# Second layer of a decoder trunk: earlier pools and loads, a one-step residual, and a later addition of R1

## The chip, the cores and the metric

The kernel runs on one core of a Trainium2 chip. The core has five engines, each with its own queue that runs in order: TensorE (PE; its weight loads are shown apart as PEld), VectorE (DVE), ScalarE (ACT), GpSimd (POOL) and SyncE (SP), which here only sends DMAs. The metric is the device time of one execution in microseconds, the median of several runs.

## The reference

A trunk of two layers over x of 512 positions by 1024 features, all in float32. Each layer is a mixer and a feed-forward part, each behind a residual and a layer norm:

```python
for layer in range(DEPTH):            # DEPTH = 2
    ...                               # layer 0: state space + stick-breaking attention; layer 1: convolution module
    x = layer_norm(DEEPNORM_ALPHA * x + mix, ln1_g[layer], ln1_b[layer])
    ffn = sqrelu_mlp(x, ffn_w1[layer], ffn_b1[layer], ffn_w2[layer], ffn_b2[layer])
    x = layer_norm(DEEPNORM_ALPHA * x + ffn, ln2_g[layer], ln2_b[layer])

def sqrelu_mlp(x, w1, b1, w2, b2):
    return jnp.square(jax.nn.relu(x @ w1 + b1)) @ w2 + b2
```

The change touches the feed-forward part of layer 1 and the norm ahead of it. There `x @ w1` has 4096 outputs, and `@ w2` goes back to 1024.

## The kernel before

Activations lie transposed, features on the 128 partitions: `X[0]` to `X[7]` are 128 features by 512 positions each. Every float32 product is made of three products of rounded halves (`hi`, `lo`): hi·hi, hi·lo, lo·hi. So each operand has to be converted first: ScalarE rounds it (`whi`, `ah`, `xdh`), VectorE takes the rest (`wlo`, `al`, `xdl`).

**Weights.** The class `Weights` holds a list of units in the order in which TensorE uses them. `_prep` loads a unit and converts it into the next of a ring of slots; `next()` hands one out and prepares a few more ahead (`W.ahead`). Some units were converted during layer 0, kept in DRAM and come back through GpSimd's DMA queue (`split`). When the first unit of the second feed-forward part's second matrix is due (`at_turn`), `turn()` closes the old pools and opens new ones: four slots, buffers for raw weights, and buffers for four quarters (`quad`, loaded by `load_quads`).

**Layer 1's feed-forward part** begins in `tail_norm_lead`. `Tail` forms the residual sums ahead of the norm, `ln_to_x` normalises the 512 positions in two halves and splits the result into `xdh`/`xdl`, and `Lead` runs the first six products with `w1` (`fl10` to `fl15`), first for the first half of the positions while the second is still being normalised, and then, in `finish`, for the second half.

Behind that come four blocks of six hidden tiles. In each, `pair` squares two tiles (`q`), forms the sums that a seven-product (Strassen) scheme needs, and splits them (`ah`, `al`). `seven` multiplies them with the four quarters of `w2` and sums of these (`operand` makes the sums on VectorE), seven units of 18 matmuls (`s`) each: 126 matmuls of 512 columns a block. Its results are added to `XT`. The first product goes into `R1[0]` and `R1[1]`, gathered over the four blocks and added to all eight `XT` at the end of the fourth. The last eight hidden tiles take an ordinary product (`h`).

In block 1, ahead of `seven`, `residual` makes alpha·x + b2: it adds `xdh` and `xdl` on VectorE, scales on ScalarE, and turns the eight tiles on TensorE (32 transposes `xt`, copied back by ScalarE), so that the output comes out with positions on the partitions.

A scheduler places each engine's instructions in order ahead of time from the order of the code and what each needs. On the chip each queue then stands at its first instruction until all that this one waits for is done. PSUM has six buffers (`nps`) that leads, transposes and `s` products take in turn.

Of the kernel before, what the change touches and what calls it, by code (L numbers as in the profile page):

```python
# [9 lines left out]
F32 = mybir.dt.float32  # L10
F32R = mybir.dt.float32r
# [5 lines left out]
P = 128  # L17
# [24 lines left out]
NB = 6  # L42
# [16 lines left out]
class Weights:  # L59
# [11 lines left out]
    def fetch(self, i):  # L71
        key, src, nk, ncol, off, width = self.units[i]
        if key not in self.chunk:
            tag, bufs = (f"quad{i % 2}{i // 2 % 2}", 1) if key[0] == "f21" else ("raw", 2)
            self.chunk[key] = self.raw.tile([P, nk, width], F32, tag=tag, name=f"raw{i}", bufs=bufs)
            self.nc.sync.dma_start(self.chunk[key], src)

    def prep_to(self, n):
# [39 lines left out]
    def load_quads(self, blk, w2, k0, nb):  # L118

        src = w2[k0 * P : (k0 + nb) * P].rearrange("(k e p) (f n) -> e f p k n", e=2, p=P, f=2)  # L120
        q = self.quads[blk] = {}
        for e, f in ((0, 0), (1, 0), (0, 1), (1, 1)):
            q[e, f] = self.raw.tile([P, nb // 2, T], F32, tag=f"quad{e}{f}", name=f"quad{blk}{e}{f}", bufs=1)
            self.nc.sync.dma_start(q[e, f], src[e, f])

    def operand(self, blk, i):
# [70 lines left out]
def kernel(ctx: ExitStack, tc: tile.TileContext, a: dict, out: bass.AP):  # L197
# [831 lines left out]
    class Lead:  # L1029


        def __init__(self, n, xs, name):
            self.n, self.xs, self.name, self.held = n, xs, name, []

        def run(self, n):
# [8 lines left out]

        def finish(self):
            self.run(self.n - len(self.held))
            n, (c0, c1) = TOGETHER.get(self.name, 0), HALVES[1]
            for k, (xh, xl) in enumerate(self.xs):
                for (hi, lo), ps in self.held[:n]:
                    for i, (u, v) in enumerate(((hi, xh), (hi, xl), (lo, xh))):  # L1050
                        PE.matmul(ps[:, c0:c1], u[:, k, :], v[:, c0:c1], start=k == 0 and i == 0, stop=k == KT - 1 and i == 2)
            for w, ps in self.held[n:]:
                gemm(ps, w, slice(0, P), self.xs, c0, c1)
            W.prep_to(W.got + 2)
            W.fence = None
            return [ps for _, ps in self.held]

    def tail_norm_lead(xk, name, bias, g, b, lead_n, lead_name, then=None):
# [7 lines left out]
        lead = Lead(lead_n, xs, lead_name)  # L1066
# [23 lines left out]
        return hs  # L1090


    rb = [const([P, KT], "rb0"), res_bias("rb1", ("ln1_b", 0), ("ffn_b2", 0)), res_bias("rb2", ("ln2_b", 0), ("conv_b_pw2", 0))]
    for n in ("ln1_g", "ln2_g", "conv_ln_g"):
        c = PV[:, vrow[n] : vrow[n] + a[n].shape[0] * KT]
        ts(c, c, -0.5, None, ALU.mult, ALU.bypass)
# [211 lines left out]

    W.ahead = AHEAD[0]

    def turn():
        wst.close()
        pools = [ctx.enter_context(tc.tile_pool(name=f"w3{x}", bufs=1, reuse_waits="tile")) for x in "abc"]
        W.slots, W.base, W.raw, W.ahead = [], W.done, pools[1], NSLOT - 1
        W.add_slots(pools[0], 2)
        W.add_slots(pools[2], NSLOT - 2)
        W.load_quads(0, a["ffn_w2"][1], 0, NB)

    W.turn = (at_turn, turn)
    xs, first = tail_norm_lead(cs_, "d", None, ("ln1_g", 8), ("ln1_b", 8), LEAD, "fl1", the_rest)  # L1320


    XT = [None] * KT
# [1 line left out]

    def residual():
        for j in range(KT):
            tt(X[j], xs[j][0].bitcast(F32), xs[j][1].bitcast(F32), ALU.add)
            act(X[j], X[j], AF.Identity, bias=pv("ffn_b2", 8 + j), scale=ALPHA)
        for f in range(2):  # L1330
            pss = [nps(f"xt{b}{f}") for b in range(4)]
            for b in range(4):
                for i in range(4):
                    PE.transpose(pss[b][:, i * P : (i + 1) * P], X[4 * f + i][:, b * P : (b + 1) * P], ident)
            for b in range(4):
                XT[2 * b + f] = X[4 * f + b]
                S.copy(X[4 * f + b], pss[b])

    hst.close()
    f1 = ctx.enter_context(tc.tile_pool(name="f1", bufs=1, side="right", reuse_waits="tile"))  # L1340
    R1 = [page(f"R1{t}", F32) for t in range(2)]

    def rect(m, ps):
# [32 lines left out]
    def seven(blk, As, first, final):  # L1376

        bank = {}
        for i in ORDER7:
# [24 lines left out]

    k0 = 0
    for bi, nb in enumerate(FFN_BLOCKS[1][:-1]):
# [5 lines left out]
        seven(k0, As, bi == 0, bi == len(FFN_BLOCKS[1]) - 2)  # L1412
        k0 += nb
    hs = []
    for i in range(nb_last):
        if i % 3 == 0:
            hl_ = [f1.tile([P, 3, T], F32R, tag=f"a{x}", name=f"b{x}{i}", bufs=NB // 2) for x in "hl"]
# [20 lines left out]
    sts = [f1.tile([P, 2, 6], F32, tag="bst", name=f"bst{b}", bufs=4) for b in range(4)]  # L1438
    pss = [nps(f"h{b}0") for b in range(4)]
    for k in range(nb_last):  # L1440
        if k % 3 == 0:
# [10 lines left out]
    ws = [W.next() for _ in range(-(-nb_last // 3))]  # L1452

    def block(b):
        mv = f1.tile([P, 4], F32, tag="bmv", name=f"bmv{b}", bufs=2)
        ps = nps(f"h{b}1")
        for k in range(nb_last):
            part(ps, b, k, ws[k // 3])
# [47 lines left out]
```

## Time and profile before

| | us |
|---|---|
| median of 3 runs (1172.56 to 1175.39) | 1173.91 |
| the profiled execution, its own time | 1172.98 |
| its span, first to last instruction | 1171.2 |
| PE busy | 1138.9 (97%) |
| PEld busy | 953.1 (81%) |
| DVE busy | 822.9 (70%) |
| ACT busy | 551.7 (47%) |

Times in the profile count from the span's start. Line numbers (L110) are those of the kernel before. Matmuls are pipelined and their ends are modelled, so a busy PE is not one at its peak; what counts is the distance between starts, and the idle time with the instruction that ended it. "Granted clock" is the share of TensorE's full clock. A view of windows gives the busy time of each engine in a stretch that the reader chooses.

### The profile page before, as it was taken

To read this page: it belongs to the slowest core of one execution; us is meant where nothing else is said; L and a number is where in the kernel's file an instruction comes from. 1 tells how busy PE (TensorE), PEld (TensorE's weight loads), DVE (VectorE), ACT (ScalarE), POOL (GpSimd) and SP (SyncE) were. 2 spreads that over 40 slices of the span, in tenths; PEclk is the share of its full clock that TensorE was granted. 3 is DMA by queue.
4 is the path that set the end of the run, shared out by engine and by line. 5 is a ranking of instruction groups with operands and counts; after the bars stand their busy time and mean duration, and the time that the engine had idled before them with its cause. 6 is when DMAs were issued, how large, how long until landed. Compare 5 with 4: busy or idle time off the path is not lost.

```text
span 1171.2 us, 17896 instructions
## 1 busy us (share of the span) xinstructions
PE 1138.9 (97%) x7180; PEld 953.1 (81%) x7180; DVE 822.9 (70%) x1396; ACT 551.7 (47%) x838; POOL 67.0 (6%) x125
## 2 busy tenths in 40 slices
PE   9989999999999999999999999899989999999997
PEld 7777767799888888888999777599968888887885
DVE  7999875498646546546555899886785958587337
ACT  7857779345425425425323132662753536363530
POOL 1022210000000000000021110001000000000000
PEclk9999999999999999999999999999989999999999
DMA  8521221332688788788454742206324151514211
GB/s 216 165 56 50 79 85 46 110 116 73 221 286 289 250 287 290 249 286 286 164 177 152 247 144 74 75 9 209 91 79 138 56 151 37 170 36 153 63 55 72
DMA packets 145907, 169.59 MB, mean 145 GB/s; under 512 B 13922, under 2 KB 119138, under 8 KB 145824
## 3 DMA queue, kind: packets, MB, share of 16 engines
q1 hardware_dynamic: 137024, 136.96, 36.7%
q0 software_dynamic: 8640, 31.46, 7.9%
q8 instruction: 56, 0.92, 0.3%
q14 instruction: 27, 0.22, 0.1%
q10 hardware_dynamic: 160, 0.03, 0.0%
HBM read 132.12 MB, written 35.65 MB: 143 GB/s over the span
## 4 chain that ended last, share of the span: by engine, by line
PE 82%; DVE 9%; ACT 4%; issue 2%; DMA 2%; POOL 0%; SPq 0%; DVEq 0%; ACTq 0%; POOLq 0%
PE f L256 24%; PE acf L256 11%; PE s L1390 8%; PE fl L256 5%; PE tlb L256 4%; PE tld L256 4%; PE h L1436 4%; PE pv L256 3%; PE pg L256 3%; PE cw L1165 3%; PE tla L256 2%; PE acmo L256 2%; PE pl L256 2%; DVE wlo L111 1%; PE gg L256 1%
## 5 line engine op out<-in xcount | busy, mean ns | idle before, releaser
L110 ACT CAST whi<-raw 128x1024 fp32r<-128x1024 f32 (+1 forms) x150 | 156.7, 1061 | 257.9 <-PE acf L256 61.0
L111 DVE TENSOR_TENSOR wlo<-raw,whi 128x1024 fp32r<-128x1024 f32 (+1 forms) x150 | 183.8, 1238 | 123.9 <-ACT whi L110 120.5
L256 PE MATMUL f<-xdh,whi 128*128 128x512 f32 x208 | 81.0, 390 | 1.0 <-ACT whi L110 1.0
L256 PE MATMUL f<-xah,whi 128*128 128x512 f32 x208 | 81.1, 390 | 0.0
L256 PE MATMUL f<-xal,whi 128*128 128x512 f32 x208 | 80.9, 389 | 0.0
L256 PE MATMUL f<-xah,wlo 128*128 128x512 f32 x208 | 80.9, 389 | 0.0
L256 PE MATMUL f<-xdl,whi 128*128 128x512 f32 x208 | 80.9, 389 | 0.0
L256 PE MATMUL f<-xdh,wlo 128*128 128x512 f32 x208 | 80.9, 389 | 0.0
L256 PE MATMUL acf<-hh,whi 128*128 128x512 f32 x192 | 75.4, 392 | 0.0
L256 PE MATMUL acf<-hh,wlo 128*128 128x512 f32 x192 | 75.2, 392 | 0.0
L256 PE MATMUL acf<-hl,whi 128*128 128x512 f32 x192 | 74.8, 390 | 0.0
L1390 PE MATMUL s<-whi,ah 128*128 128x512 f32 x168 | 66.0, 400 | 3.3 <-ACT whi L110 2.5
L1390 PE MATMUL s<-wlo,ah 128*128 128x512 f32 x168 | 66.4, 402 | 2.3 <-DVE wlo L111 2.3
L1390 PE MATMUL s<-whi,al 128*128 128x512 f32 x168 | 66.0, 396 | 0.0
L111 DVE TENSOR_TENSOR wlo<-quad,whi 128x1536 fp32r<-128x1536 f32 x28 | 49.0, 1754 | 4.7 <-ACT whi L110 4.4
L110 ACT CAST whi<-quad 128x1536 fp32r<-128x1536 f32 x28 | 41.0, 1478 | 21.9 <-PE f L256 8.0
L389 DVE SCALAR_TENSOR_TENSOR cy<-hp,wdw,cy 128x512 f32<-128x512 f32 (+1 forms) x75 | 49.5, 660 | 0.2 <-ACT cy L185 0.2
L95 POOL DMA_DIRECT2D whi<-kepth x30 | 16.1, 536 | 547.7 <-PE tlb L256 385.5
L256 PEld LDWEIGHTS f<-xdh,whi 128*128 128x128 f32 x208 | 39.0, 188 | 9.4 <-ACT whi L110 1.4
L256 PEld LDWEIGHTS f<-xah,whi 128*128 128x128 f32 x208 | 39.0, 188 | 8.2
L256 PEld LDWEIGHTS f<-xdh,wlo 128*128 128x128 f32 x208 | 39.0, 188 | 8.2
L256 PEld LDWEIGHTS f<-xah,wlo 128*128 128x128 f32 x208 | 39.0, 188 | 8.1
(649 smaller groups left out, 3069.1 us busy)
## 6 DMA issues: line engine op xcount, KB each, us to landing
raw<-in_ffn_w_dram SPq DMA_DIRECT2D x35, 1024.0 KB, 5.6
kepth<-whi SPq DMA_DIRECT2D x30, 512.0 KB, 3.4
keptl<-wlo SPq DMA_DIRECT2D x30, 512.0 KB, 9.4
whi<-kepth POOLq DMA_DIRECT2D x30, 512.0 KB, 3.6
wlo<-keptl POOLq DMA_DIRECT2D x30, 512.0 KB, 4.6
raw<-in_ffn_w_dram SPq DMA_DIRECT2D x28, 512.0 KB, 4.1
raw<-in_conv_w_pw_dram SPq DMA_DIRECT2D x12, 1024.0 KB, 7.3
quad<-in_ffn_w_dram SPq DMA_DIRECT2D x16, 768.0 KB, 4.8
```

What stands on the lines that cost most here:

```text
L95: nc.gpsimd.dma_start(x, d)
L110: i0 = nc.scalar.copy(hi, raw).ins
L111: i1 = nc.vector.tensor_sub(lo, raw, hi.bitcast(F32)).ins
L256: ins = PE.matmul(ps[:, c0:c1], u[:, k, ksl], v[:, c0:c1], start=start and k == 0 and i == 0, stop=stop and k == n - 1 and i == 2).ins
L389: V.scalar_tensor_tensor(o, x, s, y, op0=op0, op1=op1)
L1165: PE.matmul(cps[j, c0][g][C, :], Ds[j][t // 16][R, t % 16, :], hps[j][R, t + c0 : t + c1], start=t < 4, stop=t >= n - 4, tile_position=(R. ...
L1390: PE.matmul(ps, u, v[:, p, :], start=chain == i and p == 0 and n_ == 0, stop=p == len(As) - 1 and n_ == 2, skip_group_check=True)
L1436: PE.matmul(ps, u, v, start=k == 0 and i == 0, stop=k == nb_last - 1 and i == 2)
```

## The change

Five things are done.

- `finish` of the lead prepares three units (`early=3`) ahead of the second half's products instead of two behind them. So `turn()` with its loads is recorded earlier.
- `turn()` now also closes the pool of the convolution's pages (`hst`) and opens all pools of the second feed-forward part at once, over that space too: slots `s1` to `s4`, `raw`, `a0` to `a2` for the split sums, `q`, `b`, and `w` for the quarters. The quarters have a pool of their own, `W.quad`.
- The residual is one ScalarE step from the normalised value before its bias: alpha·y + (alpha·ln1_b + ffn_b2), with the bracket in a new constant `rb3`.
- `R1` is no longer added to `XT` in the last `seven`, but by one addition in each step of the loop over the last eight hidden tiles.
- The three buffers of `ah`/`al` become three pools of one each.

```diff
@@ class Weights
-            self.chunk[key] = self.raw.tile([P, nk, width], F32, tag=tag, name=f"raw{i}", bufs=bufs)
+            pool = self.quad if key[0] == "f21" else self.raw
+            self.chunk[key] = pool.tile([P, nk, width], F32, tag=tag, name=f"raw{i}", bufs=bufs)
...
-            q[e, f] = self.raw.tile([P, nb // 2, T], F32, tag=f"quad{e}{f}", name=f"quad{blk}{e}{f}", bufs=1)
+            q[e, f] = self.quad.tile([P, nb // 2, T], F32, tag=f"quad{e}{f}", name=f"quad{blk}{e}{f}", bufs=1)
@@ class Lead, finish
             self.run(self.n - len(self.held))
+            if self.early:
+                W.prep_to(W.got + self.early)
...
-            W.prep_to(W.got + 2)
+            if not self.early:
+                W.prep_to(W.got + 2)
@@
-    rb = [const([P, KT], "rb0"), res_bias("rb1", ("ln1_b", 0), ("ffn_b2", 0)), res_bias("rb2", ("ln2_b", 0), ("conv_b_pw2", 0))]
+    rb = [const([P, KT], "rb0"), res_bias("rb1", ("ln1_b", 0), ("ffn_b2", 0)), res_bias("rb2", ("ln2_b", 0), ("conv_b_pw2", 0)),
+          res_bias("rb3", ("ln1_b", 8), ("ffn_b2", 8))]
@@ turn
         wst.close()
-        pools = [ctx.enter_context(tc.tile_pool(name=f"w3{x}", bufs=1, reuse_waits="tile")) for x in "abc"]
-        W.slots, W.base, W.raw, W.ahead = [], W.done, pools[1], NSLOT - 1
-        W.add_slots(pools[0], 2)
-        W.add_slots(pools[2], NSLOT - 2)
+        hst.close()
+        f1.update((x, ctx.enter_context(tc.tile_pool(name=f"f1{x}", bufs=1, reuse_waits="tile"))) for x in "s1 s2 raw s3 a1 s4 a2 a0 q b w".split())
+        W.slots, W.base, W.raw, W.ahead = [], W.done, f1["raw"], NSLOT - 1
+        for x in ("s1", "s2", "s3", "s4"):
+            W.add_slots(f1[x], 1)
+        W.quad = f1["w"]
         W.load_quads(0, a["ffn_w2"][1], 0, NB)
@@ residual
-            tt(X[j], xs[j][0].bitcast(F32), xs[j][1].bitcast(F32), ALU.add)
-            act(X[j], X[j], AF.Identity, bias=pv("ffn_b2", 8 + j), scale=ALPHA)
+            act(X[j], X[j], AF.Identity, bias=rb[3][:, j : j + 1], scale=ALPHA)
@@
-    hst.close()
-    f1 = ctx.enter_context(tc.tile_pool(name="f1", bufs=1, side="right", reuse_waits="tile"))
@@ pair
-        q = f1.tile([P, 8, H], F32, tag="q", name=f"q{m}", bufs=2)
-        hi, lo = (f1.tile([P, 7, H], F32R, tag=f"a{x}", name=f"a{x}{m}", bufs=NB // 2) for x in "hl")
+        q = f1["q"].tile([P, 8, H], F32, tag="q", name=f"q{m}", bufs=2)
+        hi, lo = (f1[f"a{m // 2 % 3}"].tile([P, 7, H], F32R, tag=f"a{x}", name=f"a{x}{m}", bufs=1) for x in "hl")
@@ seven
-                    for x in (2 * t, 2 * t + 1, 2 * t + 4, 2 * t + 5) if final else ():
-                        tt(XT[x], XT[x], R1[t], ALU.add)
@@ the loop over the last eight hidden tiles
         split_part(*hs[-1], r)
+        tt(XT[i], XT[i], R1[i // 2 % 2], ALU.add)
```

What this does to the queues shows at three places. The first is SyncE's queue from the quarters of block 1 on (`quad000` to `quad011`, each with the semaphores that it waits for in brackets; `raw159` and `raw160` are the next weights of `w1`). Before:

```order
L124 DMA quad000_8627<-in_ffn_w2_dram 128x3x512 [waits DMAHW0_49,DVE_49]
L124 DMA quad010_8629<-in_ffn_w2_dram 128x3x512 [waits DMAHW6_49,DMAHW2_49,DVE_49]
L124 DMA quad001_8631<-in_ffn_w2_dram 128x3x512 [waits DMAHW3_49,DMASW2_49,PE_49]
L124 DMA quad011_8633<-in_ffn_w2_dram 128x3x512 [waits DMAHW4_49,DMASW3_49,PE_49]
L76 DMA raw159_8876<-in_ffn_w1_dram 128x8x128 [waits DMASW4_49,PE_49]
L76 DMA raw160_8902<-in_ffn_w1_dram 128x8x128 [waits DMASW5_49,PE_49]
```

And now:

```order
L125 DMA quad000_8510<-in_ffn_w2_dram 128x3x512 [waits DVE_49,PE_49]
L125 DMA quad010_8512<-in_ffn_w2_dram 128x3x512 [waits DMAHW2_49,PE_49]
L125 DMA quad001_8514<-in_ffn_w2_dram 128x3x512 [waits DMAHW3_49]
L125 DMA quad011_8516<-in_ffn_w2_dram 128x3x512 [waits DMAHW4_49]
L77 DMA raw159_8891<-in_ffn_w1_dram 128x8x128 [waits DMAHW0_49]
L77 DMA raw160_8917<-in_ffn_w1_dram 128x8x128 [waits DMAHW6_49]
```

The place in the queue is the same; what is waited for is not. The `PE` wait of `quad001` before names a lead product (`fl11`) that reads the weights lying there; those of `quad000` and `quad010` now name merges of the convolution (`cn`), and the other two wait for earlier DMAs alone.

The second is ScalarE's queue from the end of the lead on (`r10` to `r15` are the rectified tiles, `q` their squares, `X` from `xt` the turned residual). Before:

```order
L185 ACTIVATE r14_8686<-fl14_8418,PV_86 128x512
L1356 CAST ah2_8667<-q2_8666 128x1024
L185 ACTIVATE q4_8683<-r14_8686 128x2x256
L185 ACTIVATE r15_8689<-fl15_8447,PV_86 128x512
L185 ACTIVATE q4_8683<-r15_8689 128x512
L1356 CAST ah4_8684<-q4_8683 128x768
L1337 COPY X0_61<-xt00_8716 128x512
L1337 COPY X1_62<-xt10_8717 128x512
L1337 COPY X2_63<-xt20_8718 128x512
L1356 CAST ah4_8684<-q4_8683 128x1024
L110 CAST whi152_8635<-quad000_8627 128x1536
L1337 COPY X3_64<-xt30_8719 128x512
```

And now, from the same `r14` on:

```order
L186 ACTIVATE r14_8714<-fl14_8420,PV_86 128x512
L1363 CAST ah0_8678<-q0_8677 128x1024
L111 CAST whi154_8527<-quad000_8510 128x1536
L1363 CAST ah2_8695<-q2_8694 128x768
L1363 CAST ah2_8695<-q2_8694 128x1024
L186 ACTIVATE q4_8711<-r14_8714 128x2x256
L186 ACTIVATE r15_8717<-fl15_8449,PV_86 128x512
L1346 COPY X0_61<-xt00_8736 128x512
L186 ACTIVATE q4_8711<-r15_8717 128x512
L1346 COPY X1_62<-xt10_8737 128x512
L1363 CAST ah4_8712<-q4_8711 128x768
L1346 COPY X2_63<-xt20_8738 128x512
```

The first two quarters' casts, `whi152` and `whi153`, now stand ahead of `r10`, and the third, `whi154`, behind `r14`; in exchange casts of `ah` stand later. The eight residual steps (`X<-X,rb3`) stand between and behind the casts of `xdh`, all ahead of `whi152`.

The third is VectorE's queue in block 4's `seven`. Before, with `R10` and `R11` the two gathered first products:

```order
L385 TENSOR_TENSOR R11_8648<-R11_8648,s1811_10059 128x512
L1357 TENSOR_TENSOR al22_9970<-q22_9968,ah22_9969 128x1024
L385 TENSOR_TENSOR X0_61<-X0_61,R10_8647 128x512
L385 TENSOR_TENSOR X4_65<-X4_65,R10_8647 128x512
L385 TENSOR_TENSOR X2_63<-X2_63,R10_8647 128x512
L385 TENSOR_TENSOR X6_67<-X6_67,R10_8647 128x512
L385 TENSOR_TENSOR X1_62<-X1_62,R11_8648 128x512
L385 TENSOR_TENSOR X5_66<-X5_66,R11_8648 128x512
L385 TENSOR_TENSOR X3_64<-X3_64,R11_8648 128x512
L385 TENSOR_TENSOR X7_68<-X7_68,R11_8648 128x512
L111 TENSOR_TENSOR wlo195_10080<-quad1811_9810,whi195_10079 128x1536
L385 TENSOR_TENSOR X0_61<-X0_61,s1820_10083 128x512
```

And now:

```order
L386 TENSOR_TENSOR R11_8676<-R11_8676,s1811_10074 128x512
L1364 TENSOR_TENSOR al22_9985<-q22_9983,ah22_9984 128x1024
L112 TENSOR_TENSOR wlo195_10087<-quad1811_9825,whi195_10086 128x1536
L386 TENSOR_TENSOR X0_61<-X0_61,s1820_10090 128x512
L386 TENSOR_TENSOR X1_62<-X1_62,s1821_10100 128x512
L112 TENSOR_TENSOR wlo196_10114<-quad1801_9823,whi196_10113 128x1536
L386 TENSOR_TENSOR X6_67<-X6_67,s1850_10117 128x512
L386 TENSOR_TENSOR X7_68<-X7_68,s1851_10127 128x512
L112 TENSOR_TENSOR wlo197_10141<-quad1810_9821,whi197_10140 128x1536
```

The eight additions of `R1` stand further down, singly and in pairs between the later products' additions and the conversions `wlo198` to `wlo202`.

More of the change, by code (lines that the diff above doesn't have):

```diff
@@ L1029, with __init__ @@
     class Lead:
-        def __init__(self, n, xs, name):
+        def __init__(self, n, xs, name, early=0):
+            self.early = early
             self.n, self.xs, self.name, self.held = n, xs, name, []
@@ L1053, in finish, with tail_norm_lead @@
                 gemm(ps, w, slice(0, P), self.xs, c0, c1)
-            W.prep_to(W.got + 2)
+            if not self.early:
+                W.prep_to(W.got + 2)
             W.fence = None
             return [ps for _, ps in self.held]
-    def tail_norm_lead(xk, name, bias, g, b, lead_n, lead_name, then=None):
+    def tail_norm_lead(xk, name, bias, g, b, lead_n, lead_name, then=None, early=0):
         ln = LN(name)
@@ L1065, in tail_norm_lead @@
         xs = new_x(f"x{name}")
-        lead = Lead(lead_n, xs, lead_name)
+        lead = Lead(lead_n, xs, lead_name, early)
         ln_to_x(ln, *HALVES[0], g, b, xs, [lambda n=n: t.run(n) for n in BEFORE[:2]])
@@ L1309 @@
     W.ahead = AHEAD[0]
+    f1 = {}
     def turn():
         wst.close()
-        pools = [ctx.enter_context(tc.tile_pool(name=f"w3{x}", bufs=1, reuse_waits="tile")) for x in "abc"]
-        W.slots, W.base, W.raw, W.ahead = [], W.done, pools[1], NSLOT - 1
-        W.add_slots(pools[0], 2)
-        W.add_slots(pools[2], NSLOT - 2)
+        hst.close()
[4 more added lines that the diff above has]
+        W.quad = f1["w"]
         W.load_quads(0, a["ffn_w2"][1], 0, NB)
     W.turn = (at_turn, turn)
-    xs, first = tail_norm_lead(cs_, "d", None, ("ln1_g", 8), ("ln1_b", 8), LEAD, "fl1", the_rest)
+    xs, first = tail_norm_lead(cs_, "d", None, ("ln1_g", 8), ("ln1_b", 8), LEAD, "fl1", the_rest, 3)
     XT = [None] * KT
@@ L1374, with seven @@
     PLACE = {1: 0, 2: 1, 4: 2, 5: 3, 6: 4, 7: 5, 3: 6}
-    def seven(blk, As, first, final):
+    def seven(blk, As, first):
         bank = {}
@@ L1411 @@
             residual()
-        seven(k0, As, bi == 0, bi == len(FFN_BLOCKS[1]) - 2)
+        seven(k0, As, bi == 0)
         k0 += nb
@@ L1416 @@
         if i % 3 == 0:
-            hl_ = [f1.tile([P, 3, T], F32R, tag=f"a{x}", name=f"b{x}{i}", bufs=NB // 2) for x in "hl"]
+            hl_ = [f1[f"a{i // 3}"].tile([P, 3, T], F32R, tag=f"a{x}", name=f"b{x}{i}", bufs=1) for x in "hl"]
         r = rect(k0 + i, hidden(k0 + i))
@@ L1436, in part @@
             PE.matmul(ps, u, v, start=k == 0 and i == 0, stop=k == nb_last - 1 and i == 2)
-    sts = [f1.tile([P, 2, 6], F32, tag="bst", name=f"bst{b}", bufs=4) for b in range(4)]
+    sts = [f1["b"].tile([P, 2, 6], F32, tag="bst", name=f"bst{b}", bufs=4) for b in range(4)]
     pss = [nps(f"h{b}0") for b in range(4)]
@@ L1454, in block @@
     def block(b):
-        mv = f1.tile([P, 4], F32, tag="bmv", name=f"bmv{b}", bufs=2)
+        mv = f1["b"].tile([P, 4], F32, tag="bmv", name=f"bmv{b}", bufs=2)
         ps = nps(f"h{b}1")
```

## The prediction

> **What bounds the kernel now.** I read the chain of work that ended last first. TensorE holds most of it, so a gain has to close a hole in TensorE's stream or shorten that stream:
>
> ```profile
> PE 82%; DVE 9%; ACT 4%; issue 2%; DMA 2%; POOL 0%; SPq 0%; DVEq 0%; ACTq 0%; POOLq 0%
> ```
>
> Next I cut the second layer's feed-forward part into stages at TensorE's own boundaries. The columns are the stretch, its length, and the busy time (instructions) of PE, PEld, DVE, ACT and POOL; then the granted clock, the DMA share and GB/s.
>
> ```profile
> 847.26:853.51 6.25, 3.93 (x34) 3.38 (x33) 4.04 (x8) 5.99 (x9) 0.00 (x0) 1.00 0.00 0
> 853.51:889.14 35.63, 32.98 (x126) 25.62 (x127) 29.27 (x25) 15.30 (x17) 0.00 (x0) 0.90 0.40 118
> 983.44:1012.31 28.87, 28.87 (x127) 23.49 (x127) 24.52 (x27) 12.08 (x12) 0.00 (x0) 1.00 0.49 150
> 1044.95:1076.57 31.62, 29.88 (x130) 23.71 (x129) 28.97 (x35) 12.06 (x12) 0.00 (x0) 1.00 0.39 125
> ```
>
> The rows 853.51, 983.44 and 1044.95 are the seven-product stages (`s`) of blocks 1, 3 and 4: the same 126 matmuls each. Block 3 runs without a hole in 28.87 us, 0.229 us a matmul. Block 1 needs 35.63, that is 6.76 more. Block 4 needs 31.62; it holds two `f` matmuls of the next stage (0.46), so 2.3 is lost. The row 847.26 is the 32 transposes of the residual and a wait. The waits of line 1390 in block 1 (first two rows) and in block 4 (third) name who came last:
>
> ```profile
>   DVE wlo L111: 6.0, 6
>   ACT whi L110: 5.6, 4
>   DVE X L385: 2.0, 2
> ```
>
> In block 1 TensorE waits for the operands' conversion, in block 4 for VectorE's adds to `X`. Part of block 1's loss is the clock. Windows of 3.41 us:
>
> ```profile
> 735.69:739.11 3.42, 1.82 (x92) 1.10 (x74) 3.42 (x10) 0.00 (x0) 0.00 (x0) 1.00 0.40 141
> 739.11:742.52 3.41, 2.40 (x62) 1.31 (x62) 3.34 (x9) 1.41 (x5) 0.00 (x0) 1.00 0.03 7
> 851.74:855.16 3.42, 1.22 (x4) 0.59 (x4) 2.90 (x2) 3.42 (x5) 0.00 (x0) 1.00 0.00 0
> 855.16:858.57 3.41, 3.27 (x8) 2.59 (x9) 2.83 (x3) 2.10 (x4) 0.00 (x0) 0.50 0.00 0
> 868.81:872.22 3.41, 1.87 (x7) 0.92 (x7) 3.41 (x3) 0.71 (x1) 0.00 (x0) 1.00 0.88 254
> 872.22:875.64 3.42, 3.42 (x9) 2.63 (x9) 3.01 (x4) 0.72 (x1) 0.00 (x0) 0.50 0.60 211
> ```
>
> After a window with PE busy 1.22 of 3.42, and after one with 1.87, the next runs at clock 0.50: 8 and 9 matmuls where 14.9 fit. That costs 3.41 - 8 x 0.229 = 1.6 and 3.42 - 9 x 0.229 = 1.4, 2.9 together at most. A window with 1.82 busy (short matmuls, at 735.69) brought none, so the threshold is not sharp. Of block 1's 6.76, 2.9 is clock and some 3.9 holes.
>
> **Block 1, part by part.** The loads first.
>
> ```profile
> 765.31 0.64 PE L1185 MATMUL cn<-cq,mask 128*32 128x256 f32 x8
> 835.81 0.90 SPq L124 DMA_DIRECT2D quad<-in_ffn_w_dram  x2
> DMA to landing us min/median/max: 4.5/4.8/5.1
> 765.90:788.60 22.70, 22.70 (x185) 22.41 (x181) 17.95 (x50) 15.18 (x29) 0.00 (x0) 1.00 0.00 1
> 788.60:812.00 23.40, 23.40 (x190) 23.16 (x189) 17.66 (x46) 6.82 (x17) 6.34 (x12) 1.00 0.81 270
> ```
>
> Two of the four quarters now go out at 835.81, behind the lead products whose weights they overwrite. In the new order their last wait is for the convolution's last merge (`cn`, 765.31), so four quarters (3.1 MB) and the two weight tiles queued behind them on SP (1.0 MB) leave from 766 on. DMA is idle there (share 0.00). At the 270 GB/s of the next row 4.1 MB take about 15 us, to 781: before GpSimd's queue starts its loads at 788.6, and 50 us before the first use. SP has nothing else to send until block 2's quarters. I cost this at nothing. Without that gap it would share the engines with those loads, 4.1 MB or 15 us, still before 832.
>
> Next the residual: eight VectorE adds go, eight ScalarE steps stay but move between the second half's splits.
>
> ```profile
> 830.38 4.30 DVE L385 TENSOR_TENSOR X<-xdh,xdl 128x512 f32<-128x512 f32 x7
> 837.40 1.40 DVE L385 TENSOR_TENSOR q<-q 128x256 f32<-128x256 f32 x3 [2.72 <-ACT q L185]
> 826.34 1.31 ACT L185 ACTIVATE xdh<-X,PV 128x256 fp32r<-128x256 f32 x3 [1.06 <-DVE X L389]
> 828.71 0.91 ACT L185 ACTIVATE xdh<-X,PV 128x256 fp32r<-128x256 f32 x2 [1.06 <-DVE X L389]
> 831.17 4.41 ACT L185 ACTIVATE X<-X,PV 128x512 f32<-128x512 f32 x7 [0.67 <-DVE X L385]
> 830.14 5.76 PE fl L1051 x48
> ```
>
> The adds (4.9 us with the first) gain nothing by themselves: VectorE idles 2.72 behind them. The ScalarE steps (0.62 apart) go into two idle gaps of 1.06; four of them, 2.4 us, stand ahead of the last two splits and delay these by 0.2 to 0.4. TensorE reads the last split only near 835, at the end of the 48 products from 830.14. So all eight end near 832 instead of 835.6: cost nothing. If that cover went, the price is those 0.4 us. The new constant `rb3` is one VectorE operation of 8 columns early in the kernel, between nothing and the nearest row of its kind:
>
> ```profile
> L389 DVE SCALAR_TENSOR_TENSOR rb<-PV x2: 168/272/376, 162.7 to 162.8; 128x8 f32<-128x8 f32 x2
> ```
>
> 0.4 us at most; I take 0, since VectorE's work there is not what the second layer waits for.
>
> Now ScalarE's queue, which decides. `whi152` starts near 832 in an idle stretch. `whi153` waits for the lead's first product (835.5), takes 1.48, and pushes `r10` from 835.6 to about 836.9. Behind it stand `r11` to `r13`, which have recovered by 843, before the fifth product. From there:
>
> ```profile
> 844.58 0.69 ACT L185 ACTIVATE r<-fl,PV 128x512 f32<-128x512 f32 x1 [0.66 <-PE fl L256]
> 845.28 1.05 ACT L1356 CAST ah<-q 128x1024 fp32r<-128x1024 f32 x1
> 846.23 0.63 ACT L185 ACTIVATE q<-r 128x512 f32<-128x512 f32 x1
> 848.84 0.84 ACT L1356 CAST ah<-q 128x768 fp32r<-128x768 f32 x1
> 849.58 1.55 ACT L1337 COPY X<-xt 128x512 f32<-128x512 f32 x3
> 860.80 2.86 ACT L110 CAST whi<-quad 128x1536 fp32r<-128x1536 f32 x2
> 853.51 0.50 PE L1390 MATMUL s<-whi,ah 128*128 128x512 f32 x1 [2.15 <-ACT whi L110]
> ```
>
> In the new order ScalarE then has no gap until the third copy: `r14` 0.69, `ah0` 1.05, `whi154` 1.48, `ah2` 0.84 and 1.05, `q4` 0.63, `r15` 0.69, `X0` 0.59, `q4` 0.69, `X1` 0.59, `ah4` 0.84, `X2` 0.59: 9.73, less 0.1 for each of eleven overlaps (two casts of 1.48 take 2.86) = 8.6. From 844.58 that is 853.2, and the first `s` matmul waits for that copy, since it takes over its PSUM bank. So **the start of `s` hardly moves** (853.51 to 853.2): one wait on ScalarE takes the place of another. What goes is everything inside. At 853.2 three operand pairs are converted; `whi155`/`wlo155` are ready near 859 (five more copies 0.5 apart, a cast of 1.48, VectorE's 1.75) and needed at matmul 55 (853.2 + 54 x 0.229 = 865.6), the later ones 4 us apart with 5 or more in hand. The tightest is the third `al`: VectorE is at a subtraction of quarters until about 853.7, the `al` after it takes 0.96, and the eighth matmul wants it at 854.8; a delay there shifts all by as much. So `s` should run as in block 3: 853.2 + 28.87 = 882.1 against 889.14, **7.0 us less**, with both half-clock windows gone.
>
> **Block 4.** VectorE's row of eight adds moves behind the operands:
>
> ```profile
> 1053.94 4.90 DVE L385 TENSOR_TENSOR X<-X,R 128x512 f32<-128x512 f32 x8
> 1058.76 1.75 DVE L111 TENSOR_TENSOR wlo<-quad,whi 128x1536 fp32r<-128x1536 f32 x1
> 1072.53 0.69 DVE L385 TENSOR_TENSOR X<-X,s 128x512 f32<-128x512 f32 x1 [1.03 <-PE s L1390]
> 1074.33 1.22 DVE L111 TENSOR_TENSOR wlo<-raw,whi 128x1024 fp32r<-128x1024 f32 x1 [1.11 <-ACT whi L110]
> ```
>
> `wlo` at 1058.76 and the adds of `X` behind it come 4.9 us earlier; TensorE lost 2.3 for them, so the wait is gone with 2.6 to spare. The eight return from about 1065 on, where VectorE now has those 4.9 us and the idle 1.03 and 1.11. **2.3 us less.** A hidden cost could be that they delay a `wlo` of the next weights: bounds 0 to 2.3 given back; I take 0, as those are needed only every 24 x 0.229 = 5.5 us.
>
> **Sum.** 7.0 + 2.3 = 9.3. The profiled execution took 1172.98 (span 1171.2 and 1.8 around it): 1163.7. The median of the runs, 1173.91, lies 0.9 above: 1164.6. Had the median run only one of the two half-clock windows, 1.5 less is saved: 1166.1. I say 1165.0.
>
> **Rivals.**
> - A half-clock window stays. While ScalarE works through the queue above, TensorE does transposes piecemeal from 849.5 to 853.2, some 1.9 us idle of 3.7. A window that falls just there is about half busy, like the one at 868.81 that brought the half clock and the one at 735.69 that didn't: plus 1.5, 1166.5. Chance 0.18. The Trainium skill, "TensorE: Matmul & The Clock Gate", section "HAM oscillation — how this bites in real kernels", gives the rule that only idle gaps over about 3.4 us throttle. By it this rival could not occur and the sum is the forecast's; but the trace throttled after a longest gap of 2.15 us, so the rows decide against the rule.
> - Block 4's wait only moves: plus 2.3, 1167.3. For it speaks that VectorE's work is the same; against it, its gaps behind 1072. Chance 0.09.
> - The block 1 gain is given back at the next stage, because `f` then waits for weights: 7.0 back and 2.3 lost, no change, near 1173. Against it: their conversions follow TensorE's release of slots and shift with it. Chance 0.04.
> - Slower: ScalarE's first two casts stand ahead of `r10` in its queue, and all behind them wait if the quarters land late. Landing at L, `r10` starts at L + 2.8 instead of 836.9; 1.5 is absorbed before `r14`, so `s` slips by L - 835.6. The gain is eaten at L = 844.9. If the quarters hung on the lead's last product (847.3 + 4.8 = 852.1), the slip is 16.5, 7.2 more than the gain: 1180. Against it: the order's waits name the convolution. Chance 0.03.
>
> **How the numbers follow.** Forecast 0.66, the rivals 0.18, 0.09, 0.04, 0.03. Below 1165.0 I allow for the profiled execution's own sum, 1163.7, and 1.2 of spread between runs (half of 1172.56 to 1175.39 is 1.4): 1162.5. Above, the first two rivals together: 1168.8. About 0.2%, 2.3 us, can be told from no change: faster 0.93, same 0.04, slower 0.03.
>
> **What would show it.** Right: `quad` issues near 766; first `s` near 853, waiting for ScalarE's `X` copy; `s` of blocks 1 and 4 each about 29 us; clock 1.00 in both. Wrong: `whi152` waiting for a DMA, `s` of block 1 starting after 855, idle for `wlo` within it, or a wait moved to the `f` stages behind either block.

## The result and the profile after

| | before, us | after, us |
|---|---|---|
| median of 13 runs each | 1175.3 (1169.41 to 1178.28) | 1168.6 (1165.62 to 1174.41) |
| the profiled execution | 1172.98 | 1168.87 |
| its span | 1171.2 | 1167.2 |

The ratio of the times is 0.9947, 95% interval 0.9934 to 0.996: 4.7 to 7.8 us faster of 1175.3. The forecast was 1165.0. The sign and the upper end of the range (1168.8) hold. The medians lie 6.7 apart, 2.6 less than the sum of 9.3, and the time is 3.6 above the number forecast.

The page's chain of work that ended last had 82% PE, 9% DVE, 4% ACT and 2% DMA before. After, less of it lies on VectorE (the shares listed now add up to 88% only, so the row is no measure of the gain):

```profile
PE 78%; ACT 4%; DMA 3%; DVE 2%; issue 1%; POOL 0%; SPq 0%; DVEq 0%; ACTq 0%
```

The view of windows in the kernel after, cut as in the prediction into the transposes with their wait and then the seven products, here of blocks 1, 2 and 4:

```profile
852.88:858.74 5.86, 4.14 (x35) 3.38 (x33) 5.86 (x7) 5.86 (x11) 0.00 (x0) 1.00 0.00 0
858.74:887.65 28.91, 28.91 (x127) 23.92 (x128) 22.62 (x24) 13.37 (x16) 0.00 (x0) 1.00 0.50 150
920.30:949.12 28.82, 28.82 (x127) 23.49 (x127) 24.49 (x27) 12.07 (x12) 0.00 (x0) 1.00 0.51 151
1043.22:1072.04 28.82, 28.82 (x127) 23.49 (x127) 28.46 (x34) 12.06 (x12) 0.00 (x0) 1.00 0.47 140
```

All three product stages now take 28.8 to 28.9 us with TensorE busy throughout and the clock at 1.00. Block 1 was 35.63, block 4 31.62. The waits of TensorE's matmuls from the lead's end to the last matmul, before:

```profile
PE s L1390 <- ACT whi L110: 2.5, 2, 2.2
PE s L1390 <- DVE wlo L111: 2.3, 3, 1.2
PE f L256 <- ACT whi L110: 1.0, 1, 1.0
PE s L1390 <- DVE X L385: 0.8, 1, 0.8
PE xt L1334 <- ACT X L1337: 0.2, 1, 0.2
```

and after (total us, times, longest):

```profile
PE xt L1343 <- ACT r L186: 0.8, 1, 0.8
PE s L1397 <- ACT X L1346: 0.6, 1, 0.6
PE xt L1343 <- ACT X L1346: 0.3, 1, 0.3
```

The one wait left ahead of `s`, for ScalarE's copy `X`, is the one that the prediction named. ScalarE's row of work ahead of it (start, length, instruction, idle time before it) in the kernel after:

```profile
850.21 0.69 ACT L186 ACTIVATE r<-fl,PV 128x512 f32<-128x512 f32 x1 [1.53 <-PE fl L257]
...
855.89 0.57 ACT L1346 COPY X<-xt 128x512 f32<-128x512 f32 x1
856.36 0.64 ACT L186 ACTIVATE q<-r 128x512 f32<-128x512 f32 x1
856.89 0.58 ACT L1346 COPY X<-xt 128x512 f32<-128x512 f32 x1
857.35 0.85 ACT L1363 CAST ah<-q 128x768 fp32r<-128x768 f32 x1
858.09 1.09 ACT L1346 COPY X<-xt 128x512 f32<-128x512 f32 x2
```

From `r14` at 850.21 to the first `s` at 858.74 are 8.5 us without a gap; 8.6 had been worked out. The loads leave where the order had them, behind the convolution (SP's queue; the upstream part of this execution is some 5 us later, so 772 stands for 766):

```profile
771.99 2.40 SPq L125 DMA_DIRECT2D quad<-in_ffn_w_dram  x4
774.43 5.10 SPq L77 DMA_DIRECT2D raw<-in_ffn_w_dram  x2
```

Now the whole stretch in which the change was to pay, from the lead's last product to the last matmul, before and then after:

```profile
847.42:1163.16 315.74, 309.03 (x1352) 252.13 (x1350) 215.62 (x245) 138.37 (x157) 0.00 (x0) 0.99 0.30 91
```

```profile
853.05:1159.08 306.03, 304.31 (x1352) 250.41 (x1350) 210.88 (x243) 135.83 (x158) 0.00 (x0) 1.00 0.31 94
```

It is 9.7 us shorter; 9.3 had been forecast. But the two rows also show that the lead's end itself comes 5.6 us later (853.05 against 847.42). So in these two executions the gain was made where it was expected, and over half of it is lost again ahead of the code that the change is about. The experiments ask why.

### The profile page after: what moved, and what is told of

Read it like the earlier page. It is cut to its first block, busy times and chain, and to the rows that moved or that the text cites. A ratio compares the mean times of both kernels' runs of the same rounds, so it can differ in the third digit from the quotient of the medians.

```text
span 1167.2 us, 17873 instructions
## 1 busy us (share of the span) xinstructions
PE 1137.1 (97%) x7180; PEld 952.1 (82%) x7180; DVE 816.3 (70%) x1389; ACT 550.0 (47%) x838; POOL 66.2 (6%) x125
## 4 chain that ended last, share of the span: by engine, by line
PE 78%; ACT 4%; DMA 3%; DVE 2%; issue 1%; POOL 0%; SPq 0%; DVEq 0%; ACTq 0%
PE f L257 21%; PE acf L257 10%; PE s L1397 10%; PE fl L257 5%; PE tld L257 4%; PE h L1442 4%; PE tlb L257 4%; PE pv L257 3%; DMA raw<-in_ffn_w_dram 3%; PE pg L257 3%; PE cw L1171 3%; PE tla L257 2%; PE acmo L257 2%; PE pl L257 2%; PE gg L257 1%
## 5 line engine op out<-in xcount | busy, mean ns | idle before, releaser
L257 PEld LDWEIGHTS f<-xal,whi 128*128 128x128 f32 x208 | 39.0, 188 | 8.1
L257 PEld LDWEIGHTS f<-xdl,whi 128*128 128x128 f32 x208 | 39.0, 188 | 8.1
```

The lines of the kernel that those rows point to most:

```text
L257: ins = PE.matmul(ps[:, c0:c1], u[:, k, ksl], v[:, c0:c1], start=start and k == 0 and i == 0, stop=stop and k == n - 1 and i == 2).ins
```

## The experiments

The table gives, for one profiled execution of each version, the distance from the first `acf` matmul (layer 0's second feed-forward product) to the first `tlb` matmul, the lead's end, the distance from there to the last matmul, and how many half-clock windows (stretches of 3.41 us with a granted clock of about 0.5) lie in that last stretch. The ratio is that of the timed runs to the kernel before, run beside them.

| version | `acf` to `tlb` | lead's end at | lead's end to last matmul | half-clock windows there | ratio, 95% interval |
|---|---|---|---|---|---|
| before | 263.51 | 847.42 | 315.74 | 2 | |
| same | 264.47 | 851.88 | 314.17 | 1 | 0.9998 (0.9978 to 1.0018) |
| r1_move_alone | 263.83 | 855.28 | 311.93 | 1 | 1.0003 (0.9984 to 1.0022) |
| before_with_filler | 264.21 | 850.69 | 312.79 | 0 | 0.9987 (0.9972 to 1.0002) |
| one_step_residual_alone | 264.83 | 856.81 | 317.36 | 1 | one run |
| after | 264.83 | 853.05 | 306.03 | 0 | 0.9947 (0.9934 to 0.996) |
| after_again | 265.52 | 852.36 | 306.05 | 0 | 0.9945 (0.9926 to 0.9965) |
| no_r1_move | 265.40 | 856.99 | 310.01 | 1 | 0.998 (0.9962 to 0.9998) |
| two_step_residual_again | 265.16 | 856.06 | 306.65 | 0 | one run |
| rb3_in_old_columns | 263.51 | 850.48 | 306.10 | 0 | 0.9919 (0.9893 to 0.9945) |
| rb3_old_columns_again | 263.51 | 856.42 | 306.05 | 0 | 0.9936 (0.9921 to 0.9951) |
| rb3_in_64_bytes | 262.96 | 849.33 | 305.97 | 0 | one run |
| residual_one_product_later | 264.83 | 851.58 | 303.92 | 0 | 0.9939 (0.992 to 0.9959) |
| later_residual_old_columns | 263.50 | 850.53 | 303.93 | 0 | 0.9892 (0.987 to 0.9914) |

**The unchanged kernel again.** No edit.

> The kernel before, unchanged, to see what two profiled executions of one kernel differ by. Theory P (the gain lies in blocks 1 and 4 alone; half-clock windows there depend on where the free-running 3.41 us windows fall): ratio 1.000 within 0.2%; the stretch up to the end of the lead products differs from the first profile by as much as the changed kernel's did (some 3 to 6 us), and block 1 has 0 to 2 half-clock windows, its seven products taking 32.5 to 35.6 us. Theory U (the change itself slows what runs ahead of the lead): the end of the lead products lies within 1 us of the first profile's 847.3.

Its ratio is 1 within its interval, but its profiled execution reached the lead's end 4.5 us later than the first one did. The profiled execution on which the prediction's sum stood had the earliest lead's end of all fourteen in the table. Block 1 fell otherwise on the windows of 3.41 us, and had one half-clock window instead of two. Two neighbouring windows of 3.41 us in block 1 of this execution:

```profile
856.85:860.26 3.41, 1.72 (x6) 1.05 (x7) 2.71 (x2) 3.41 (x5) 0.00 (x0) 1.00 0.00 0
860.26:863.67 3.41, 3.41 (x9) 2.67 (x9) 3.38 (x2) 2.05 (x5) 0.00 (x0) 0.51 0.00 0
```

After a window in which TensorE was busy 1.72 of 3.41, the next had half the clock: 9 matmuls where 14.9 fit. So the stretch costs 315.74 with two such windows, 314.17 with one. Measured against this second execution, the change gains 8.1 us there instead of 9.7.

**R1 added later, alone.** The kernel before, with

```diff
-                    for x in (2 * t, 2 * t + 1, 2 * t + 4, 2 * t + 5) if final else ():
-                        tt(XT[x], XT[x], R1[t], ALU.add)
...
         split_part(*hs[-1], r)
+        tt(XT[i], XT[i], R1[i // 2 % 2], ALU.add)
```

> The kernel before with only the later addition of R1. By the prediction: block 4's seven products fall from 31.6 to 29.3 (with the two f matmuls among them), nothing else moves, 2.3 us less, ratio 0.998. Rival (the wait only moves): 1.000.

With one half-clock window each, the stretch went from 314.17 to 311.93: 2.2 us, for 2.3 forecast. The timed ratio does not show it: 1.0003, an interval that would just admit 2 us. In its profiled execution 10.24 us at half clock fell into layer 0's mixer, and the granted clock of its twelve timed runs was 0.990 in the mean, against 0.991 in those of the kernel before. Its windows just before and in that stretch:

```profile
150.27:153.69 3.42, 3.42 (x21) 3.00 (x20) 3.42 (x6) 1.17 (x2) 0.04 (x1) 1.00 0.20 57
153.69:157.10 3.41, 1.38 (x13) 1.18 (x11) 3.41 (x5) 1.72 (x4) 2.38 (x1) 1.00 0.05 7
157.10:167.34 10.24, 7.00 (x20) 3.92 (x21) 2.60 (x5) 3.08 (x7) 2.64 (x3) 0.50 0.18 52
```

TensorE stood idle there for 4.4 us, from the second of these windows into the third; what it waited for is shown further down.

**The change without the R1 move.** The same lines the other way round, in the kernel after.

> The changed kernel with R1 added in the last seven-product stage again, as before. If the move of R1 is worth 2.3 us as the prediction has it: the seven products of block 4 take 31.1 us instead of 28.8, ratio 0.9967. Rival (the wait only moves): block 4 and the stage behind it together take as long as in the changed kernel, ratio 0.9947.

310.01 against 306.03, with one half-clock window in block 4. There TensorE waits twice, as before the change: an `f` matmul of the next stage, which stands among the `s` in the order, for ScalarE's `whi`, and an `s` matmul for VectorE's adds. The waits of block 4, then the two windows of that execution:

```profile
PE f L257 <- ACT whi L111: 1.0, 1, 1.0
PE s L1397 <- DVE X L386: 0.8, 1, 0.8
```

```profile
1062.96:1066.37 3.41, 1.69 (x7) 0.76 (x6) 3.41 (x5) 1.04 (x1) 0.00 (x0) 1.00 0.67 202
1066.37:1069.78 3.41, 3.41 (x8) 2.66 (x9) 3.41 (x5) 0.00 (x0) 0.00 (x0) 0.51 0.92 272
```

The window costs 3.41 less 8 x 0.229, 1.6; the other 2.4 are the R1 move. Its price is nearly the same from both sides. What the prediction missed for block 4 is that such a hole carries a second price, paid only in those executions whose windows fall on it.

**Filler in the holes.** The kernel before, with 20 matmuls into an unused PSUM bank:

```diff
+    def fill(n):
+        ps = stp("fill")
+        for i in range(n):
+            PE.matmul(ps, negs, xs[0][0], start=i == 0, stop=i == n - 1)
...
         if bi == 0:
             residual()
+            fill(9)
...
+            if first and i in FILL:   # FILL = {5: 4, 6: 7}
+                fill(FILL[i])
```

> The kernel before with 20 matmuls into an unused PSUM bank, placed where TensorE waits in block 1 (9 behind the residual, 4 and 7 ahead of the products of units 5 and 6); their results are not used. Theory A (the half-clock windows of block 1 follow from windows of 3.41 us that were only about half busy, and cost 1.4 to 1.6 each): granted clock 1.00 through block 1, no window at half clock between the lead's end and block 2, and from the first `xt` to the last matmul 313.0 (the 312.9 that two executions with windows leave when 1.5 is taken off for each: 315.9 with two, 314.4 with one), that is 1.4 to 2.9 less than before although 20 matmuls more run; the median 1 to 2 us under before. Rival B (the clock falls for another reason, such as power or chance): a half-clock window in block 1 as often as before, and 2 us or more longer where a filler does not fit its hole.

No half-clock window is left in block 1, and from the first `xt` to the last matmul it takes 313.0, as expected, though it executes 20 matmuls more. Block 1's windows (transposes and filler, then the products) in this kernel:

```profile
850.69:856.79 6.10, 5.93 (x42) 4.99 (x40) 3.88 (x8) 6.00 (x9) 0.00 (x0) 1.00 0.00 0
856.79:888.00 31.21, 29.99 (x131) 24.08 (x131) 27.42 (x24) 15.20 (x16) 0.00 (x0) 1.00 0.46 135
```

The mean granted clock of its 12 timed runs is 0.994, as in the kernel after; that of the 17 runs of the kernel before beside them is 0.991. So the half-clock windows follow from the holes, not the other way round, and the clock alone explains 1.4 to 2.9 us of the gain. The timed median is 1.6 lower, with an interval that takes in no change.

**The change again, and with `rb3` in old columns.** For the second:

```diff
-          res_bias("rb3", ("ln1_b", 8), ("ffn_b2", 8))]
+          res_bias("rb3", ("ln1_b", 8), ("ffn_b2", 8), PV[:, :KT])]
```

where `res_bias` writes into the columns that it is given, which nothing reads any more, instead of a page of its own.

> The changed kernel with its new constant rb3 written into columns of PV that are no longer read, so that every tile lies at the address that it had before. Theory P: ratio to the kernel before 0.9947 as for the changed kernel, within 0.15%. Theory U, in the form that the 32 bytes of rb3 move every later tile and cost time upstream: about 0.992, 3 us better than the changed kernel.

> The changed kernel again, for its ratio on this chip and for a second execution with a profile. From the first lead transpose's predecessor on (the residual's transposes `xt` to the last matmul) the first profile of it took 306.2 us with no half-clock window. Theory C (the stages behave as the prediction says, and the rest of the shortfall is half-clock windows and delays that differ from execution to execution): the same stretch takes 306.2 plus 1.5 per half-clock window in it, the ratio lies at 0.993 to 0.996, and the start of `xt` lies anywhere from 847 to 857. Theory U (the changed kernel is itself later ahead of the second layer, by the new constant rb3 and the addresses that it moves): start of `xt` at 852 or later again, ratio 0.9945 or above, and the version with rb3 in old columns 2 us or more below it.

> The changed kernel with rb3 in columns of the vectors' page that are no longer read, so that no address differs from before; in the first series it had only six runs. Theory C: ratio to before within 0.2% of the repeated changed kernel's. Theory U: at least 0.2% (2.3 us) below it, and start of `xt` below 851 again (850.3 the first time).

By the start of `xt` that these expectations named, the new constant looks innocent: its second execution in old columns came to `xt` at 856.3, later than either execution of the change. That measure was too coarse, since the lead's end scatters by 9.6 us over the executions in the table. Cut by stage it is not innocent. The `acf` stretch, before:

```profile
307.50:571.01 263.51, 263.51 (x1162) 216.73 (x1161) 141.28 (x155) 108.36 (x128) 0.00 (x0) 1.00 0.79 270
```

after:

```profile
309.07:573.90 264.83, 264.83 (x1162) 216.72 (x1160) 138.94 (x153) 107.08 (x125) 0.00 (x0) 1.00 0.79 268
```

and after, with `rb3` in old columns:

```profile
309.03:572.54 263.51, 263.51 (x1162) 216.71 (x1161) 141.31 (x156) 108.22 (x128) 0.00 (x0) 1.00 0.79 270
```

The same 1162 matmuls, TensorE never idle, the clock full, and 1.3 us more. The view of one line shows where (shortest, median and longest duration in ns, first and last start), before and after:

```profile
L256 PE MATMUL acf<-hl,whi x192: 388/389/393, 307.7 to 527.0; 128*128 128x512 f32 x192
```

```profile
L257 PE MATMUL acf<-hl,whi x192: 389/395/403, 309.3 to 529.9; 128*128 128x512 f32 x192
```

These matmuls take 6 ns longer in the median. Their median is 395 in each of the six executions with `rb3` in 32 bytes of its own, and 389 in each of the eight others. So the stretch takes 264.8 or more in the six and 264.5 or less in the eight, where the two highest, 264.47 and 264.21, have waits of 0.2 for `hl` and 0.3 to 0.4 for `hh`. The timed medians of the two pairs differ by 1.9 us (1168.6 and 1166.7) and 0.6 (1168.07 and 1167.45); the intervals of the ratios overlap in both, so the timed runs alone do not show it.

The scatter of the lead's end has another source. Over half of it goes with one GpSimd operation of layer 0's mixer, `w2B`; behind it GpSimd makes the `w2C` for which TensorE waits. Two executions of the same kernel, `rb3` in old columns, the first and then the second, with the wait in each:

```profile
155.25 0.49 POOL L705 TENSOR_SCALAR_AFFINE_SELECT w2B<-w2B 128x256 f32<-128x256 f32 x1 [4.42 <-ACT w2B L192]
PE av L756 <- POOL w2C L705: 2.1, 2, 1.2
```

```profile
155.14 4.06 POOL L705 TENSOR_SCALAR_AFFINE_SELECT w2B<-w2B 128x256 f32<-128x256 f32 x1 [4.39 <-ACT w2B L192]
PE av L756 <- POOL w2C L705: 5.3, 2, 4.5
```

It takes 4.0 to 4.1 us in five executions (`r1_move_alone`, `one_step_residual_alone`, `no_r1_move`, `two_step_residual_again`, `rb3_old_columns_again`) and 0.5 in the nine others. The five have 6.8 to 10.2 us at half clock behind it and reach the lead's end at 855.28 or later, the nine at 853.05 or earlier. One kernel shows both, so it does not take an edit; why it happens was not tried. It does not separate the first two profiles, which both have 0.5. Of the 5.6 us between their lead's ends, 1.3 are `acf`. Of the rest, 1.2 lie ahead of 58 us, 1.4 in the stage behind `acf` and 1.6 in the convolution, stages that differ from execution to execution as well (56.6 to 58.3, 48.1 to 49.5 and 91.5 to 95.3).

**`rb3`'s page in 64 bytes, and the one-step residual alone.** The first is the kernel after with

```diff
-          res_bias("rb3", ("ln1_b", 8), ("ffn_b2", 8))]
+          res_bias("rb3", ("ln1_b", 8), ("ffn_b2", 8), const([P, 2 * KT], "rb3")[:, :KT])]
```

the second the kernel before with `rb3` and

```diff
-            tt(X[j], xs[j][0].bitcast(F32), xs[j][1].bitcast(F32), ALU.add)
-            act(X[j], X[j], AF.Identity, bias=pv("ffn_b2", 8 + j), scale=ALPHA)
+            act(X[j], X[j], AF.Identity, bias=rb[3][:, j : j + 1], scale=ALPHA)
```

> The changed kernel with rb3's page 64 bytes a partition instead of 32, half of it unused. If the longer acf stretch comes from operands that are off by an odd 32 bytes (theory D1), it is 263.5 again; if any shift does it, or a shift relative to a larger unit (D2), it stays at 264.8 or takes a third value. From the lead's end to the last matmul 306.0 either way.

> The kernel before with two things of the change alone: the residual in one ScalarE step and, for it, the new constant rb3 in a page of its own, 32 bytes a partition, ahead of most other tensors. Theory D (rb3's page moves the operands of the first layer's feed-forward products by 32 bytes, and these run longer there; the step itself gains nothing): from the first `acf` matmul to the first `tlb` 264.8 us or a few tenths more, where every execution without rb3's own page took 263.5 to 264.5; from the lead's end to the last matmul 312.7 plus 1.5 per half-clock window, as before (315.7 with two, 314.2 with one). Rival E (the acf stretch is longer for another part of the change, or by chance): 263.5 there. Rival F (the eight VectorE adds were on the path): 1 to 4.9 us less behind the lead's end.

In 64 bytes the stretch is 262.96, even 0.5 below the kernel before:

```profile
309.02:571.98 262.96, 262.96 (x1162) 216.69 (x1160) 140.71 (x155) 108.45 (x128) 0.00 (x0) 1.00 0.80 271
```

So with 0 and with 64 bytes more ahead of them the matmuls are short, and with 32 long: it is the place of what lies behind `rb3` that counts, not the operation that makes it. The other run shows `acf` at 264.83 as expected, and missed behind the lead's end: 317.36, where one half-clock window gives 314.2. Its products of block 2 take

```profile
929.85:959.34 29.49, 29.49 (x127) 23.48 (x126) 24.90 (x27) 11.91 (x12) 0.00 (x0) 1.00 0.48 147
```

against, in the unchanged kernel run again,

```profile
924.75:953.60 28.85, 28.85 (x127) 23.50 (x126) 24.66 (x27) 11.92 (x12) 0.00 (x0) 1.00 0.48 149
```

again with no wait. A third of the `s` matmuls of all four blocks, those of `wlo` and `ah`, with the one-step residual and then in the unchanged kernel; the median is 396 ns where it was 389:

```profile
L1390 PE MATMUL s<-wlo,ah x168: 389/396/796, 864.7 to 1085.9; 128*128 128x512 f32 x168
```

```profile
L1390 PE MATMUL s<-wlo,ah x168: 388/389/629, 859.8 to 1079.1; 128*128 128x512 f32 x168
```

Blocks 1 to 4 lose 0.2, 0.6, 0.6 and 0.3, the last product `h` 1.3 (44.95 for 43.68). So in this one execution 32 bytes in the old arrangement of pools go with a loss of 3.2 us in the second layer besides the 1.3 in the first; the page and the step were not tried apart there. The new arrangement is spared that: its `s` stages are 28.7 to 28.9 with `rb3` in either place.

**The residual in two steps again.** The same two lines the other way round, in the kernel after.

> The changed kernel with the residual in two steps again (eight VectorE adds, then ScalarE), rb3 still made. Theory A (the adds are covered: VectorE idles there, and ScalarE has recovered before the first `s`): from the lead's end to the last matmul 306.0 to 306.5, against 306.0 in the changed kernel. Rival F (the adds hold up ScalarE's steps, and these its queue up to the first `s`): 307 to 311. The acf stretch at 264.8 as long as rb3 has its own page.

306.65, 0.15 above what was allowed and 0.6 above the kernel after; a wait of 0.3 for `al` is new. The eight VectorE adds were all but covered, as costed.

```profile
PE s L1398 <- DVE al L1365: 0.3, 1, 0.3
```

**The residual one product later,** and then this together with `rb3` in old columns:

```diff
-        if bi == 0:
-            residual()
...
                     tt(XT[x], XT[x], ps, ALU.add)
+            if first and i == 1:
+                residual()
```

> The changed kernel with the residual's eight ScalarE steps, 32 transposes and eight copies moved behind the first of block 1's seven products, so that `s` need not wait for the copies in ScalarE's queue. Theory A (what delays the first `s` is that queue, as the prediction has it): first `s` about 5 us after the lead's end instead of 5.9 after the first `xt`, and the stretch from the lead's end to the last matmul about 2 us shorter than in the changed kernel (304.2 against 306.2 at full clock), ratio to before 0.992. Rival B (the queue only moves: the copies then stand ahead of the casts that block 1's middle products need, or the transposes make the same hole later): within 0.5 us of the changed kernel. Rival C: slower by 1.5 or more, since the hole makes a new half-clock window.

> The two versions that beat the changed kernel in their stretch, together: the residual behind the first of block 1's seven products, and rb3 in columns of the vectors' page that are no longer read. Theory (the two gains are independent): acf stretch 263.5, no wait of TensorE between the lead's end and the first `s`, 303.9 from the lead's end to the last matmul, and at equal clock 3.4 us less than the changed kernel, so a ratio to before of 0.990 to 0.993. Rival (executions differ ahead of the second layer by so much that it does not show): 0.993 to 0.995.

If ScalarE's queue is what delays the first `s`, it need not wait for the copies. It does not: in the first of the two, `s` starts as the lead ends, the transposes run between the products, and 303.92 is 2.1 under the kernel after, with no wait at all:

```profile
851.58:1155.50 303.92, 303.92 (x1352) 250.18 (x1351) 210.53 (x243) 135.97 (x158) 0.00 (x0) 1.00 0.31 94
```

Timed alone it is not distinguishable from the change (0.9939, 0.992 to 0.9959), where 0.992 was expected. Both edits together give a median of 1162.78 (6 runs, before beside it 1175.47), ratio 0.9892 (0.987 to 0.9914): faster than both kernels. Its stages are the expected ones (263.50 and 303.93). The ratio is below the expected 0.990 to 0.993: the distance to the change's 0.9947 is some 6 us, where the two stages explain 3.4. The surplus stays open.

## Which steps of the prediction held, and which failed

- **Block 1, forecast 7.0.** `s` 28.91 for 28.87 forecast; its start 5.69 behind the lead's end where it was 6.09, so 0.4 earlier for 0.3 forecast; the wait ahead of it is the forecast's, for the third copy. Right, and moving the residual shows that ScalarE's queue was the cause.
- **Block 4, forecast 2.3.** 2.2 alone and 2.4 taken from the change. Right in size. The prediction put all of it down to VectorE's adds; 1.0 is the wait of an `f` matmul for `whi`, and it goes with the same move.
- **Residual, costed at nothing.** 0.6 better than the old form within the new order, in one execution. Nearly right.
- **`rb3`, costed at 0 to 0.4 and taken as 0.** This step failed. The prediction looked up the length of the VectorE operation and reasoned that the second layer does not wait for it. It did not ask what a page of 32 bytes does to the tensors placed behind it. That cost 1.3 us in layer 0, in a stage at which the prediction had not looked, over three times the upper bound.
- **The half-clock windows, 2.9 of block 1's 7.0.** This term was taken too large. The mechanism was right (the filler shows it), but the size is not the same in each execution: of the four profiled executions with block 1's old holes, one had two windows there and three had one. The number forecast, 1165.0, leaned on two (1164.6) rather than one (1166.1). The rival that a window stays in block 1 did not come true in any of the nine executions with the new order.
- **The anchor.** The median of three runs, 1173.91, was 1.4 below that of the 13 beside the change, and other series gave 1175.2 to 1175.6. The lead's end of the profiled execution was the earliest seen.
- **The waits of line 1390.** The 6.0 and 5.6 us that the prediction showed count the idle time of weight loads and matmuls together, so they add up to more than the 6.76 that block 1 lost. The matmuls alone waited 2.3 and 2.5. The sum did not use these figures.

The account for 1168.6 against 1165.0 is made afterwards: 1.4 for the anchor, 1.3 for `rb3`'s page, 1.1 if a typical execution has one window (1166.1 less 1165.0), less 0.4 of stage that came out better: 3.4 of 3.6. That the terms nearly add up is no proof. The third term is not settled. The granted clock rose from 0.991 to 0.994 in the mean of the timed runs, which is about two windows (0.003 of 1170 is 3.5 us, a window at half clock 1.7), not one. That mean also counts windows ahead of the lead, and in how many timed runs `w2B` took long is not known. It also stays open whether `rb3`'s page costs more than 1.3 ahead of the second layer. The lead's end lies at 854.5 in the mean of the six executions with it and 851.5 in the eight without. Where `w2B` took 0.5 us, the means are 852.3 (three) and 850.1 (six); where it took 4.1, they are 856.6 (three) and 855.9 (two). So the difference is 0.8 to 2.3 between executions that are alike in this, and the 1.3 lies within that.

The rule weighed in the prediction (the Trainium skill, "TensorE: Matmul & The Clock Gate", section "HAM oscillation — how this bites in real kernels", that only idle gaps over about 3.4 us throttle) does not agree with the windows shown above: half clock followed such with 1.69 and 1.72 us busy of 3.41, which leaves at most 1.7 us in them for an idle gap.

## What to carry to other kernels

A small new constant is an edit to the address of everything placed behind it: compare the durations of the same matmuls in untouched stages before and after, and put such a page where nothing moves; 64 bytes instead of 32 did as well here, in one execution. Where a hole in TensorE's stream leaves it about half busy for a few microseconds, count the hole as certain and the half-clock window behind it as something that only part of the executions pay. A single profiled execution is no anchor for a change of half a per cent: profile the unchanged kernel again, cut both into stages, and take the time of each where it repeats to the tenth.

## What the runs showed of the hardware

- The same matmuls, with no wait and the clock at 1.00, take 389 ns in the median or 395 to 396, according to whether a page of 32 bytes a partition lies ahead of their operands; a block of 126 takes 29.49 us instead of 28.85, 5 ns more each. With 64 bytes it does not grow (one execution). Which operand counts, and whether writes of other engines take part, was not tried. The Trainium skill, "SBUF — State Buffer", section "Operand start alignment", asks only for a multiple of the element size and says that its runs timed nothing; here 32 bytes are such a multiple, and the time differs.
- Half clock came in steps of 3.41 us: one after a window busy for 1.69 to 1.72, and three in a row (10.24) in layer 0's mixer after one busy for 1.38, in which an idle gap of 4.4 us began.
- The same GpSimd affine select of 128x256 took 0.49 us in one execution and 4.06 in another of the same kernel.
